# Loading attention's values and later keys, queries and biases from POOL's queue in a one-core hybrid block

## The chip, the core and the metric

The kernel runs on one core of one Trainium2 chip. The metric is the device time of one execution in microseconds (us). A profile of one execution gives the time of every instruction on each engine: TensorE (PE, with its weight loads as PEld), VectorE (DVE), ScalarE (ACT), GpSimd (POOL), and the queue of SyncE (SP), which only starts transfers. Transfers can be started from SP, from ACT and from POOL; they are carried out by the core's 16 DMA engines.

## The reference

One layer of a diffusion backbone over 512 latent tokens (a grid of 8 rows of 64 columns) and 256 context tokens, width 1024. The tokens are normalised and projected; half of the width goes to attention over a neighbourhood and the context (8 heads of 64), the other half to a recurrent scan over time in both directions. Their outputs are joined, projected and added; then a mixture of 32 experts follows. The part at hand, cut:

```
px, pc = hx @ w_in, hc @ w_in
qx, kx, vx = na_heads(px[..., :3 * D_NA], ...)      # latent tokens
qc, kc, vc = na_heads(pc[..., :3 * D_NA], ...)      # context tokens
s_win = (q @ k_band) * scale + bias                 # band of 8 x 32 tokens for 8 x 16 queries
s_ctx = (q @ kc) * scale
p = softmax(concat([s_win, s_ctx]))
o = p[window] @ v_band + p[context] @ vc
```

## The kernel before

The kernel is written in a tile framework: tiles come from pools, the framework places the semaphores, and a planner chooses each queue's order from the program's order and its own estimate of times. Instructions that are pinned (`pin`, or all of TensorE's while `strict` is set) keep the program's order among themselves.

The projections come first. They end with the attention's last values (`nv1`) and queries. Values go to a tensor in memory (NVd, 768 tokens by 512) from ACT's queue; queries (QTd) and keys (KTd) go to memory from SP's, each as a rounded part and a remainder (z = 0, 1).

Then `scan_and_attention` runs two things together on TensorE. The scan has 12 steps (`scan_step(j)`); at the end of step j `scan_load(j + 2)` loads four kinds of tile from SP, into two buffers each, in this order: BKj (pinned, 512 KB), ARz (two halves), UVj (two), TTj. In step j the matmuls `pr`, then `pu`, then `pgr` (which reads BKj and ARz of step j + 1), `pds`, `pgr` again, and the transposes `pkb` (BKj of step j + 1, its last reader). In the gaps of each step the attention is fed in from a generator (`other_work`), in the program's order. The attention has 16 units (`u`): four pairs of heads p, four column blocks cb each. For each unit and head there are the scores `psc` (6 matmuls of k and q), the bias and softmax on VectorE and ScalarE, the transposes `ppt`, and, one unit later, the product with the values `pon` (16 matmuls for both heads).

Its inputs come in two places. `att_values` loads nine V tiles of 128 x 512 (256 KB): seven overlapping bands of the grid, 16 columns of each of the 8 rows, and two of context. Unit 0 uses V0, V2, V7 and V8, the first four issued. `att_load(p)` loads for one pair of heads k, q (rounded), k, q (remainder) and two bias tiles `bt`, 2.0 MB in all; for p = 0 before the scan starts, for p = 1, 2, 3 at the units 2, 6, 10. Even and odd pairs have their own set of buffers. The first two calls also clear the fourth part of `bt` on POOL.

After the attention comes the output projection, with its weights (`wo`, from SP) multiplied by a gate on POOL and split into two parts (`woh`, `wol`), while the scan ends; then the experts, whose weights (384 loads of 512 KB) stream from SP to the end.

Of the kernel before, what the change touches and what calls it, by code (L numbers as in the profile page):

```python
# [226 lines left out]
class K:  # L227
# [1008 lines left out]
    def att_values(s):  # L1236
        nc, PN = s.nc, s.PN
        s.V = {}
        for a in (0, 2, 1, 3, 5, 4, 6):
            s.V[a] = PN.tile([128, 512], F32, name=f"V{a}")  # L1240
            nc.sync.dma_start(s.V[a], s.NV[0:512].rearrange("(r c) f -> r c f", c=64)[:, 8 * a:8 * a + 16])
            if a == 2:
                for b in range(2):
                    s.V[7 + b] = PN.tile([128, 512], F32, name=f"V{7 + b}")
                    nc.sync.dma_start(s.V[7 + b], s.NV[512 + 128 * b:640 + 128 * b])

    def att_load(s, p):

        nc, P = s.nc, s.pns[p % 2]
        t = []  # L1250
        for z in range(2):
            k = P.tile([128, 768], F32, name=f"k{z}")
            s.pin(nc.sync.dma_start(k, s.KTd[p, z]))
            q = P.tile([128, 512], F32, name=f"q{z}")
            nc.sync.dma_start(q, s.QT[p, z])
            t.append((q, k))
        for h in range(2):
            if p < 2:
                s.bt.append(P.tile([128, 4, 256], F32, name=f"bt{h}"))
                nc.gpsimd.memset(s.bt[-1][:, 3], 0.0)  # L1260
            nc.sync.dma_start(s.bt[2 * (p % 2) + h][:, 0:3], s.A['bias'][2 * p + h])
        return t

    def attention(s):
# [730 lines left out]
```

## Time and profile before

| | |
|---|---|
| median of 3 runs | 1205.52 us (1205.4 to 1206.56) |
| the profiled execution's own time | 1203.45 us |
| its span, first to last instruction | 1201.7 us |
| mean granted TensorE clock | 0.956 of full speed |
| TensorE busy | 1105.2 us (92%) |
| VectorE, ScalarE, POOL busy | 658.4, 393.5, 249.6 us |
| DMA moved | 309.98 MB, mean 258 GB/s |

Rows of a timeline give the start, the duration, the engine, the operation with its output and inputs, how many were merged, and in brackets the idle time before and what ended it. The duration of a DMA on a queue is the time to issue it, not to move the data. [...]

### The profile page before, as it was taken

What the parts mean: (1) busy time and instruction counts of PE and PEld (TensorE: products, weight loads), DVE (VectorE), ACT (ScalarE), POOL (GpSimd) and SP (SyncE); (2) the same over time, 40 slices, a digit from 0 to 9 for tenths busy, and PEclk for the clock granted to TensorE, in tenths of its full rate; (3) what the DMA queues carried; (4) which work ended last, traced back from release to release, by engine and by line L of the source; (5) the groups of instructions that cost most, each with busy time, mean ns of one, the idle gap of its engine ahead of it and who ended that gap; (6) DMA issues with size and microseconds to landing.
All of it is one profiled execution on the core that took longest, in us unless ns stands there. A gap on an engine that the chain in (4) does not pass through costs nothing.

```text
span 1201.7 us, 23662 instructions
## 1 busy us (share of the span) xinstructions
PE 1105.2 (92%) x9545; PEld 761.2 (63%) x9546; DVE 658.4 (55%) x1461; ACT 393.5 (33%) x743; POOL 249.6 (21%) x277
## 2 busy tenths in 40 slices
PE   3899988997996798999997979999999999999996
PEld 1677776775764777888775754646464646464644
DVE  5645589659699823554467782333333333333335
ACT  3533551643555344555312252202021111111200
POOL 0654554535244210020135140000000000000000
PEclk9999988997798898999999989999999999999998
DMA  9544634663462488764333939999999999999995
GB/s 366 175 131 128 188 128 137 169 209 98 120 180 102 125 240 220 220 177 107 111 105 101 379 140 352 409 408 409 409 409 409 408 409 408 409 409 409 409 409 187
DMA packets 148764, 309.98 MB, mean 258 GB/s; under 512 B 32291, under 2 KB 71075, under 8 KB 148652
## 3 DMA queue, kind: packets, MB, share of 16 engines
q1 hardware_dynamic: 143868, 306.08, 71.7%
q10 hardware_dynamic: 4752, 2.36, 0.7%
q8 instruction: 76, 1.25, 0.4%
q14 instruction: 36, 0.29, 0.1%
q0 software_dynamic: 32, 0.00, 0.0%
HBM read 283.22 MB, written 25.17 MB: 257 GB/s over the span
## 4 chain that ended last, share of the span: by engine, by line
PE 68%; DVE 21%; DMA 6%; ACT 2%; issue 2%; POOL 1%; SPq 0%; ACTq 0%; DVEq 0%; POOLq 0%
PE ph L242 17%; PE py L242 9%; PE psc L242 7%; PE ipn L242 5%; PE pga L242 5%; PE ip L242 5%; DVE tmp L212 4%; DVE Tc L212 4%; PE pgr L242 2%; DMA wt<-in_w_dram 2%; PE pm L242 2%; PE acc L242 2%; PE pr L242 2%; PE pon L242 1%; PE ppt L246 1%
## 5 line engine op out<-in xcount | busy, mean ns | idle before, releaser
L242 PE MATMUL ph<-wt,HS 128*64 128x512 f32 x1024 | 224.1, 593 | 0.2 <-DMA wt<-in_w_dram 0.2
L242 PEld LDWEIGHTS ph<-wt,HS 128*64 128x64 f32 x1024 | 73.4, 137 | 140.2 <-issue 126.1
L212 DVE TENSOR_TENSOR hid<-hid,ph 128x512 f32<-128x512 f32 x16 | 11.0, 688 | 249.3 <-PE ph L242 249.3
L242 PE MATMUL py<-wt,hid 128*64 128x256 f32 x1024 | 114.5, 381 | 0.0
L242 PEld LDWEIGHTS py<-wt,hid 128*64 128x64 f32 x1024 | 71.9, 137 | 40.3 <-issue 3.9
L212 POOL CAST two<-sel 128x128 fp32r<-128x128 f32 x32 | 8.6, 297 | 425.7 <-PE pbc L242 425.7
L212 POOL TENSOR_TENSOR wlo<-wraw,whi 128x512 fp32r<-128x512 f32 x54 | 74.3, 1378 | 70.2 <-ACT whi L212 67.7
L242 PE MATMUL ipn<-whi,hth 128*128 128x256 f32 x256 | 79.4, 310 | 5.9 <-DVE vs L212 4.8
L212 DVE TENSOR_TENSOR x<-psc,x 128x512 f32<-128x512 f32 (+1 forms) x136 | 78.5, 648 | 0.0
L242 PE MATMUL ip<-hth,whi 128*128 128x512 f32 (+1 forms) x200 | 76.5, 383 | 0.2 <-ACT nr L212 0.2
L242 PE MATMUL ipn<-wlo,hth 128*128 128x256 f32 x256 | 74.7, 292 | 0.0
L242 PE MATMUL ipn<-whi,htl 128*128 128x256 f32 x256 | 74.6, 291 | 0.0
L242 PE MATMUL ip<-htl,whi 128*128 128x512 f32 (+1 forms) x200 | 72.9, 364 | 0.7 <-DVE htl L212 0.7
L242 PE MATMUL ip<-hth,wlo 128*128 128x512 f32 (+1 forms) x200 | 72.5, 363 | 0.0
L242 PEld LDWEIGHTS ipn<-whi,hth 128*128 128x128 f32 x256 | 51.4, 201 | 17.8 <-issue 14.8
L242 PE MATMUL pga<-OH,xh 128*128 128x256 f32 x240 | 60.4, 292 | 0.9 <-DVE OH L212 0.9
L242 PE MATMUL pga<-OH,xl 128*128 128x256 f32 x240 | 59.5, 288 | 0.0
L212 DVE TENSOR_TENSOR tmp<-Mc,Tc 128x30 f32<-128x30 f32 (+14 forms) x120 | 56.8, 473 | 4.8 <-ACT Tc L212 3.2
L242 PE MATMUL psc<-yh,oht 128*128 128x512 f32 (+1 forms) x136 | 54.6, 405 | 1.2 <-DVE x L212 0.8
L212 DVE TENSOR_TENSOR Tc<-Tc,tmp 128x30 f32<-128x30 f32 (+14 forms) x120 | 52.3, 436 | 2.0
L242 PEld LDWEIGHTS ip<-hth,whi 128*128 128x128 f32 x200 | 39.9, 199 | 21.0 <-issue 15.7
L212 ACT ACTIVATE hid<-pth 128x512 f32<-128x512 f32 x16 | 9.6, 599 | 132.7 <-PE pth L246 132.7
(352 smaller groups left out, 2279.6 us busy)
## 6 DMA issues: line engine op xcount, KB each, us to landing
wt<-in_w_dram SPq DMA_DIRECT2D x384, 512.0 KB
wm<-in_wmod_dram SPq DMA_DIRECT2D x48, 512.0 KB
wraw<-in_w_in_dram SPq DMA_DIRECT2D x30, 256.0 KB
wraw<-in_w_na_dram SPq DMA_DIRECT2D x24, 256.0 KB
BKj<-BKd SPq DMA_DIRECT2D x12, 512.0 KB
BKd<-BK SPq DMA_DIRECT2D x12, 384.0 KB
ARz<-ARd SPq DMA_DIRECT2D x16, 256.0 KB
wo<-in_w_out_dram SPq DMA_DIRECT2D x16, 256.0 KB
```

The source lines that it names most:

```text
L212: i = f(*a, **k)
L242: i = s.nc.tensor.matmul(out, l, r, start=start, stop=stop)
L246: i = s.nc.tensor.transpose(out, x, s.ident if ident is None else ident)
```

## The change

Twenty-seven loads name another queue. The nine V loads go from SP to POOL. The six loads of a pair of heads go to POOL for the second, third and fourth pair; the first pair's stay on SP. Sizes, buffers, the order in the program and all other loads are as before.

```
         for a in (0, 2, 1, 3, 5, 4, 6):
             s.V[a] = PN.tile([128, 512], F32, name=f"V{a}")
-            nc.sync.dma_start(s.V[a], s.NV[0:512].rearrange("(r c) f -> r c f", c=64)[:, 8 * a:8 * a + 16])
+            nc.gpsimd.dma_start(s.V[a], s.NV[0:512].rearrange("(r c) f -> r c f", c=64)[:, 8 * a:8 * a + 16])
             if a == 2:
                 for b in range(2):
                     s.V[7 + b] = PN.tile([128, 512], F32, name=f"V{7 + b}")
-                    nc.sync.dma_start(s.V[7 + b], s.NV[512 + 128 * b:640 + 128 * b])
+                    nc.gpsimd.dma_start(s.V[7 + b], s.NV[512 + 128 * b:640 + 128 * b])
...
     def att_load(s, p):
         nc, P = s.nc, s.pns[p % 2]
+        q1 = nc.sync if p == 0 else nc.gpsimd
         t = []
         for z in range(2):
             k = P.tile([128, 768], F32, name=f"k{z}")
-            s.pin(nc.sync.dma_start(k, s.KTd[p, z]))
+            s.pin(q1.dma_start(k, s.KTd[p, z]))
             q = P.tile([128, 512], F32, name=f"q{z}")
-            nc.sync.dma_start(q, s.QT[p, z])
+            q1.dma_start(q, s.QT[p, z])
             t.append((q, k))
         for h in range(2):
...
-            nc.sync.dma_start(s.bt[2 * (p % 2) + h][:, 0:3], s.A['bias'][2 * p + h])
+            q1.dma_start(s.bt[2 * (p % 2) + h][:, 0:3], s.A['bias'][2 * p + h])
         return t
```

## Rows read from the trace of the kernel before

**Rows 1.** The page: busy time (share of span) and instructions; one DMA queue's packets.

```profile
PE 1105.2 (92%) x9545; PEld 761.2 (63%) x9546; DVE 658.4 (55%) x1461; ACT 393.5 (33%) x743; POOL 249.6 (21%) x277
...
q0 software_dynamic: 32, 0.00, 0.0%
```

**Rows 2.** Windows: length, busy time (instructions) per engine, granted clock, DMA share, GB/s.

```profile
440.00:445.00 5.00, 4.44 (x58) 3.59 (x58) 3.15 (x9) 3.72 (x7) 0.00 (x0) 1.00 0.65 159
440.00:458.40 18.40, 14.61 (x202) 11.44 (x201) 9.04 (x26) 10.96 (x22) 0.00 (x0) 0.99 0.83 203
...
449.90:472.20 22.30, 17.10 (x225) 14.79 (x224) 7.86 (x21) 8.61 (x18) 0.00 (x0) 0.85 0.94 233
472.20:487.30 15.10, 15.10 (x225) 13.01 (x224) 8.47 (x23) 10.02 (x21) 0.00 (x0) 1.00 0.55 153
470.00:584.00 114.00, 114.00 (x1695) 96.59 (x1693) 58.23 (x152) 65.45 (x129) 8.15 (x10) 1.00 0.57 156
740.00:760.00 20.00, 20.00 (x122) 8.62 (x119) 4.01 (x7) 1.86 (x3) 0.00 (x0) 1.00 1.03 409
```

**Rows 3.** Timeline of TensorE's matmuls, 432 to 507 us.

```profile
432.23 0.66 PE L246 MATMUL pkb<-cst,BKj 128*128 128x128 f32 x4
...
446.31 1.96 PE L242 MATMUL pon<-PT,V 128*64 128x128 f32 x12
448.54 0.44 PE L242 MATMUL pon<-PT,V 128*64 128x128 f32 x4 [0.27 <-DMA V<-NVd]
...
460.86 1.30 PE L242 MATMUL pgr<-ARz,BKj 128*64 128x128 f32 x5 [5.20 <-DMA BKj<-BKd]
...
462.43 2.07 PE L242 MATMUL pon<-PT,V 128*64 128x128 f32 x13
...
470.18 1.09 PE L242 MATMUL pon<-PT,V 128*64 128x128 f32 x16
...
474.39 0.97 PE L242 MATMUL psc<-k,q 64*128 64x256 f32 x6
...
506.58 0.97 PE L242 MATMUL psc<-k,q 64*128 64x256 f32 x6
```

**Rows 4.** The chain that ended last, in order of time, 440 to 461 us.

```profile
440.85 6.42 DMA V<-NVd
447.29 13.43 DMA BKj<-BKd
```

**Rows 5.** Timeline of SP's queue, 438 to 485 us.

```profile
438.16 1.55 SPq L212 DMA_DIRECT2D ARz<-ARd  x2
440.14 5.65 SPq L212 DMA_DIRECT2D V<-NVd  x9
447.29 0.32 SPq L212 DMA_DIRECT2D BKj<-BKd  x1
...
453.13 0.33 SPq L212 DMA_DIRECT2D k<-KTd  x1
...
460.74 1.30 SPq L212 DMA_DIRECT2D bt<-in_bias_dram  x2
...
484.80 0.43 SPq L212 DMA_DIRECT2D k<-KTd  x1
```

**Rows 6.** Waits of SP's queue, 584 to 665 us: total us, times, longest.

```profile
SPq L212 <- POOL wol L212: 25.4, 5, 6.4
```

**Rows 7.** Timeline of POOL, 437 to 516 us.

```profile
512.60 2.51 POOL L212 TENSOR_TENSOR wo<-wo,g 128x512 f32<-128x512 f32 x2 [75.73 <-DMA wo<-in_w_out_dram]
```

**Rows 8.** Waits of all engines, 395 to 590 us: total us, times, longest.

```profile
PEld pon L242 <- DMA V<-NVd: 1.1, 3, 0.5
```

**Rows 9.** Instructions on tensor cntd, the one transfer issued from POOL.

```profile
L212 POOL DMA_DIRECT2D cntd<-hid x1: 669/669/669, 719.1 to 719.1; - x1
...
DMA to landing us min/median/max: 3.9/3.9/3.9
```

**Rows 10.** Two loads issued from SP: ns of the issue, min/median/max.

```profile
L212 SPq DMA_DIRECT2D brow<-in_bge_dram x1: 283/283/283, 586.6 to 586.6; - x1
...
L212 SPq DMA_DIRECT2D V<-NVd x9: 430/572/669, 440.1 to 445.2; - x9
```

More of the change, by code (lines that the diff above doesn't have):

```diff
@@ L1240, in att_values @@
             s.V[a] = PN.tile([128, 512], F32, name=f"V{a}")
-            nc.sync.dma_start(s.V[a], s.NV[0:512].rearrange("(r c) f -> r c f", c=64)[:, 8 * a:8 * a + 16])
+            nc.gpsimd.dma_start(s.V[a], s.NV[0:512].rearrange("(r c) f -> r c f", c=64)[:, 8 * a:8 * a + 16])
             if a == 2:
@@ L1244, in att_values @@
                     s.V[7 + b] = PN.tile([128, 512], F32, name=f"V{7 + b}")
-                    nc.sync.dma_start(s.V[7 + b], s.NV[512 + 128 * b:640 + 128 * b])
+                    nc.gpsimd.dma_start(s.V[7 + b], s.NV[512 + 128 * b:640 + 128 * b])
     def att_load(s, p):
         nc, P = s.nc, s.pns[p % 2]
+        q1 = nc.sync if p == 0 else nc.gpsimd
         t = []
@@ L1252, in att_load @@
             k = P.tile([128, 768], F32, name=f"k{z}")
-            s.pin(nc.sync.dma_start(k, s.KTd[p, z]))
+            s.pin(q1.dma_start(k, s.KTd[p, z]))
             q = P.tile([128, 512], F32, name=f"q{z}")
-            nc.sync.dma_start(q, s.QT[p, z])
+            q1.dma_start(q, s.QT[p, z])
             t.append((q, k))
@@ L1260, in att_load @@
                 nc.gpsimd.memset(s.bt[-1][:, 3], 0.0)
-            nc.sync.dma_start(s.bt[2 * (p % 2) + h][:, 0:3], s.A['bias'][2 * p + h])
+            q1.dma_start(s.bt[2 * (p % 2) + h][:, 0:3], s.A['bias'][2 * p + h])
         return t
```

## The prediction

> **What bounds the kernel now.** I read the page's engine list first: TensorE is busy for 92% of the span and GpSimd (POOL) for 21% [rows 1]. Averages over stages say nothing about one edit, so next I cut the span into windows [rows 2]. Around the edit the reader is to see two things. From 470 to 584 us TensorE is busy 114.00 of 114 us at full clock: there no load is waited for. Before that, 449.9 to 472.2 and 472.2 to 487.3 hold the same number of matmuls, 225, being two consecutive scan steps with the same attention work between them; the first takes 22.3 us, the second 15.1 us. So about 7.2 us are lost in the first step.
>
> The TensorE timeline says where: 5.20 us of idle time at 455.7, ended by the load of a BKj tile, and slow matmuls behind it (13 matmuls of `pon` take 2.07 us, where 16 of the next group take 1.09) [rows 3]. [...] Hence 7.2 = 5.2 idle + 2.0 at the lower clock.
>
> Why was BKj late? In the chain that ended last, its load takes 13.43 us from 447.29, and before it stands the landing of a V load, 6.42 us from 440.85 [rows 4]. The SP queue's own timeline makes it plain [rows 5]: after the nine V at 440.14 the queue no longer issues freely. BKj goes out when the second V has landed (440.85 + 6.42 = 447.27), eight issues after it. Behind BKj come two UVj, TTj, k, q, k, q and then, eight issues after BKj, `bt` at 460.74, just as BKj lands (447.29 + 13.43 = 460.72). So on SP an issue waits until the load eight places ahead of it has landed.
>
> **The change part by part.**
>
> *V leaves SP.* BKj stands next behind two ARz issues that end at 439.7. The load eight places before it is then one issued before 430, long landed, and the buffer's last reader, the transposes `pkb`, ended at 432.9 [rows 3]. I take the issue at 439.7 instead of 447.3. Even if it again needed 13.4 us it would land at 453.1, before TensorE asks for it at 455.7; it is late again only if it takes longer than the present 13.4 us (rival B). So the wait goes: **-7.2 us**, with the lower clock that followed it. The UVj and TTj behind it go earlier too; TensorE waits for neither today.
>
> *V goes to POOL.* POOL is idle for 75.73 us up to 512.60 [rows 7], so V and the loads behind it delay no arithmetic before the multiplication of `wo`, which serves the output projection after 584. But V itself is on the path: the first `pon` group (16 matmuls from 446.31 to 448.98) takes 2.7 us where a later one takes 1.09, because its weight loads wait for V tiles, three times, 1.1 us in all, the matmuls a little more [rows 3, 8]; the fourth V lands just before the last four matmuls, at about 448.5. Anything that delays the fourth V beyond 448.5 stops TensorE.
>
> What does an issue from POOL cost? The trace has only one, a row of 0.1 KB: 0.67 us, 3.9 us to landing [rows 9]. Lower bound: 0.67 each. Upper: in proportion to packets; that queue moved 32 packets in all [rows 1], a V tile has 128 rows, so 2.7 us. Between them: SP took 0.283 us for a 0.1 KB load and 0.572 for a V [rows 10], a factor of 2.0, which gives 1.35 us on POOL. I take that, since the form differs less from SP's than a plain proportion supposes. Four V are then issued at 440.1 + 5.4 = 445.5, against 442.7 (nine in 5.65 us). If they land as long behind their issue as now (5.9 us for the fourth), the delay is 2.9 us; if only the time behind an issue that the one POOL row shows (3.2 us) and 0.6 us of transfer remain, it is 0.8. BKj is now under way in the same time, 0.5 MB; the DMA share is 0.65 in 440 to 445 [rows 2], so there is room for part of it. I take **+2.0 us**; bounds -1.6 (the present stall gone, since 0.65 leaves room) and, at 2.7 us an issue, 4 x 2.7 - 2.5 = +8.3 (2.5 being what four issues take now).
>
> *k, q and bias of the second pair.* On POOL, behind the nine V. They are first used at 474.4 [rows 3], after the change about 469. Without BKj, UVj and TTj before them they can follow V directly; if POOL too waits eight issues back, k goes when the second V has landed, some 4 us earlier than at present (453.1), and the biases at about 457 instead of 460.7. Some 10 us are left: 0. SP's next BKj no longer stands behind them.
>
> *Third and fourth pair.* The third is issued from 484.80 [rows 5] and first used at 506.58 [rows 3]: 20 us of TensorE's work hide it, and the fourth likewise: 0. SP gets the room, and needs it nowhere, as TensorE does not wait from 470 on.
>
> *Does it last to the end?* From 470 to 584 time is set by TensorE alone, and later the expert weights run at 409 GB/s with all engines busy [rows 2], a stage that begins when TensorE has got there. A shift at 470 should pass to the end undiminished.
>
> Sum: -7.2 + 2.0 = -5.2. The profiled execution took 1203.45 (span 1201.7); it becomes 1198.25. The runs' median is 1205.52, 2.07 above it; so 1205.52 - 5.2 = **1200.3**.
>
> **The rivals.**
>
> *A. V comes sooner, 1196.7.* From 440 to 458.4 the core moved 203 x 18.4 = 3.7 MB [rows 2], while what had landed by then, nine V and two ARz, is 2.6 MB. So 1.1 MB of loads issued later had passed them: V used only part of the engines' width. On another queue that may spread better, and the stall of 1.6 us at 446 goes too: -7.2 - 1.6. [...]
>
> *B. The engines, not the queue, make BKj late: 1205.5.* If V and BKj share so badly that BKj is served last, it lands when all this data has moved, again at about 460.7, and the wait stays. For: the DMA share of 0.94 in that step [rows 2]. Against: 1.1 MB of later loads did pass V, and 0.5 MB at 203 GB/s are 2.6 us. [...]
>
> *C. Slower: POOL writes its loads too slowly.* Place: the first `pon` group. With t us an issue the fourth V is late by 4t - 2.5, and a stall of some us brings the low clock again (2.0). Break-even at t = 1.9; slower by over 2.4 us from t = 2.5. At 2.7: -7.2 + 8.3 + 2.0 = +3.1, 1208.6. [...] Against: the one row of 0.67. [...]
>
> *D. The planner writes another order.* VectorE, ScalarE and SP are ordered by a planner in the output projection; there SP waits 25.4 us for the product `wol`, 6.4 at most once [rows 6]. One more such wait: -5.2 + 6.4 = +1.2, 1206.7.
>
> **How the numbers follow.** What a measurement of this kernel can tell from no change is about 0.2%, 2.4 us. Forecast 0.47, A 0.17, B 0.13, C 0.12, D 0.11 (half of it beyond 2.4 us). Faster: forecast and A, 0.64; same: B and half of D, 0.19; slower: C and half of D, 0.17. The range runs from just under A to just short of C: 1196.5 to 1208. The likeliest case alone: 1198.5 to 1203.
>
> **What would show it.** Right: BKj issued on SP near 440 and no wait of TensorE for it; two steps of nearly equal length; a clock near 1.00 from 450 to 472; V issues on POOL of 1 to 1.5 us; the first `pon` group at 4 to 5 us. Wrong: POOL issues of 2 us or more, with `pon` stopped for longer than 5 us; BKj landing after 455; a wait for `bt` or `k` near 468; or a gain at 470 that is smaller at 660, which would be the planner's.

## The result, and the profile after

The changed kernel takes 1212.95 us (median; 1211.51 to 1213.56) against 1205.46 of the kernel before in the same measurement: ratio 1.0058, 95% interval 1.0036 to 1.008, so 7.5 us slower. The forecast was 1200.3 us and the range ended at 1208.0. The profiled execution took 1211.51 us with a span of 1209.7 us, 8.0 us more than the span before.

What the change was to remove is gone. SP's queue after the change, timeline from 439 to 456 us:

```profile
439.50 0.53 SPq L212 DMA_DIRECT2D BKj<-BKd  x1
440.12 0.38 SPq L212 DMA_DIRECT2D TTj<-TTd  x1
440.74 0.32 SPq L212 DMA_DIRECT2D g<-gated  x1
441.11 1.07 SPq L212 DMA_DIRECT2D wo<-in_w_out_dram  x2
442.29 0.49 SPq L212 DMA_DIRECT2D x<-in_x_dram  x1
443.60 1.39 SPq L212 DMA_DIRECT2D UVj<-VDd  x2
445.03 0.61 SPq L212 DMA_DIRECT2D x<-in_x_dram  x1
455.62 0.33 SPq L212 DMA_DIRECT2D BKj<-BKd  x1
```

BKj goes out at 439.50 and not at 447.29 [rows 5], and TensorE no longer waits for it. But the queue does not stay empty. The gate's vector (`g`, 512 KB), two tiles of output weights (`wo`, 256 KB each) and two of `x` (256 KB each) leave at once, 1.5 MB that serve the output projection, more than 100 us later. In the kernel before, `g` was issued only at 469.75, `wo` at 505.84 and `x` at 511.01.

POOL's queue after the change, timeline from 440 to 470 us:

```profile
440.01 4.98 POOL L212 DMA_DIRECT2D V<-NVd  x8 [14.23 <-DMA QTd<-nx]
447.27 0.59 POOL L212 DMA_DIRECT2D V<-NVd  x1 [2.28 <-DMA V<-NVd]
450.77 0.57 POOL L212 DMA_DIRECT2D k<-KTd  x1 [2.91 <-DMA V<-NVd]
...
465.28 0.54 POOL L212 DMA_DIRECT2D bt<-in_bias_dram  x1 [7.68 <-issue]
...
466.61 2.50 POOL L212 TENSOR_TENSOR wo<-wo,g 128x512 f32<-128x512 f32 x2
```

Eight V take 4.98 us to issue, 0.62 each. Then POOL stands still too: the ninth V, k, k and q each wait for a V to land, and arithmetic queued behind them (the product of `wo` with the gate) comes at 466.61. On the first bias load two views differ: the list of V below puts its 7.7 us on V, the timeline on nothing that it shows (`issue`). Eight places ahead of it stands the sixth V, which by the trace's semaphores had landed at 458.8, 6.5 us before this issue; what held POOL for those 6.5 us stays open. V itself lands late. All instructions on V after the change; first who waited for V (us, times), then issue to landing:

```profile
  POOL bt L212: 7.7, 1
...
  PE pon L242: 5.5, 4
...
DMA to landing us min/median/max: 7.0/13.9/19.7
```

TensorE's matmuls after the change:

```profile
447.03 0.44 PE L242 MATMUL pon<-PT,V 128*64 128x128 f32 x4 [1.16 <-DMA V<-NVd]
450.27 0.44 PE L242 MATMUL pon<-PT,V 128*64 128x128 f32 x4 [2.80 <-DMA V<-NVd]
451.12 0.70 PE L242 MATMUL pon<-PT,V 128*64 128x128 f32 x4 [0.41 <-DMA V<-NVd]
452.99 0.70 PE L242 MATMUL pon<-PT,V 128*64 128x128 f32 x4 [1.18 <-DMA V<-NVd]
```

The first `pon` group stops four times, for 5.5 us, where before it stopped for 0.3 [rows 3]. Windows after the change (columns as in [rows 2]):

```profile
440.00:458.40 18.40, 12.59 (x138) 9.91 (x140) 5.21 (x16) 7.25 (x15) 8.08 (x14) 0.79 1.03 245
...
456.00:458.00 2.00, 2.00 (x38) 1.88 (x38) 0.00 (x0) 0.46 (x1) 0.86 (x2) 0.50 1.15 205
...
464.00:466.00 2.00, 2.00 (x31) 1.88 (x30) 0.33 (x2) 0.00 (x0) 0.72 (x2) 0.50 1.01 387
...
455.50:477.00 21.50, 20.75 (x225) 18.05 (x224) 8.81 (x22) 9.21 (x19) 8.07 (x13) 0.72 1.06 237
477.00:492.20 15.20, 15.20 (x228) 13.07 (x226) 8.54 (x24) 10.13 (x21) 1.03 (x2) 1.00 1.05 255
```

The DMA share in 440 to 458.4 is 1.03 instead of 0.83 [rows 2]. And the step from 455.5, with the same 225 matmuls, is busy for 20.75 of 21.50 us: it waits for almost nothing, yet takes 6.4 us more than the step that needs 15.1 [rows 2]. Its granted clock, a share of full speed, is 0.72: behind the stops for V the clock is 0.50, and stays there while TensorE is busy 2.00 of every 2 us. So 5.65 of the 6.4 us are longer busy time, and 0.75 one wait:

```profile
469.21 0.66 PE L246 MATMUL ppt<-cst,S 128*128 128x128 f32 x4 [0.75 <-ACT S L212]
```

So a pair of losses took the place of the one removed. I count from the start of the `pr` matmuls that read UVj, one group in each step. The table holds every profiled run (first step: the one with the first `pon` group; second: the next; "last V": start of the last four `pon` matmuls of the first group, from the first step's start; empty where they do not stand by themselves).

| kernel | first step | second | third | last V |
|---|---|---|---|---|
| before | 17.11 | 22.30 | 15.10 | 15.72 |
| before, again | 17.30 | 21.88 | 15.11 | 15.90 |
| after | 23.21 | 21.52 | 15.11 | 20.68 |
| after, again | 25.64 | 20.98 | 15.11 | 23.12 |
| values only (e1) | 23.87 | 20.22 | 15.10 | 21.34 |
| keys, queries, biases only (e2) | 24.07 | 20.08 | 15.11 | 21.55 |
| after, other loads held (e3) | 19.49 | 20.82 | 15.11 | 16.97 |
| e3, TensorE kept busy (e5) | 20.53 | 16.37 | 15.10 | 19.13 |
| after, TensorE kept busy (e6) | 24.14 | 29.67 | 15.11 | 22.75 |
| e6, `wo` held (e9) | 24.54 | 15.26 | 26.30 | 23.14 |
| before, BKj ahead of V (e4) | 19.04 | 15.10 | 15.11 | |
| before, BKj fifth (e7) | 16.50 | 15.11 | 18.58 | 15.11 |
| e4, TensorE kept busy (e10) | 17.58 | 15.12 | 16.36 | |

After against before: first step +6.1, second -0.8, together +5.3. In the second pair of profiles it is +8.3 and -0.9, together +7.4.

### The profile page after: what moved, and what is told of

It is laid out like the page before. It is cut to its first block, busy times and chain, and to the rows that moved or that the text cites. A ratio compares the mean times of both kernels' runs of the same rounds, so it can differ in the third digit from the quotient of the medians.

```text
span 1209.7 us, 23692 instructions
## 1 busy us (share of the span) xinstructions
PE 1107.9 (92%) x9545; PEld 763.3 (63%) x9546; DVE 661.2 (55%) x1461; ACT 393.6 (33%) x743; POOL 267.8 (22%) x304
## 4 chain that ended last, share of the span: by engine, by line
PE 66%; DVE 20%; DMA 7%; issue 2%; ACT 2%; POOL 2%; SPq 0%; DVEq 0%; ACTq 0%; POOLq 0%
PE ph L242 17%; PE py L242 8%; PE psc L242 6%; PE ipn L242 6%; PE pga L242 5%; PE ip L242 5%; DVE tmp L212 4%; DVE Tc L212 4%; DMA wt<-in_w_dram 3%; PE pgr L242 2%; PE pm L242 2%; PE acc L242 2%; PE pr L242 1%; PE ppt L246 1%; DMA V<-NVd 1%
## 5 line engine op out<-in xcount | busy, mean ns | idle before, releaser
L242 PEld LDWEIGHTS ipn<-whi,hth 128*128 128x128 f32 x256 | 51.3, 200 | 18.1 <-issue 15.1
```

The costliest lines, as they stand in the source:

```text
L242: i = s.nc.tensor.matmul(out, l, r, start=start, stop=stop)
```

## The experiments

The first four runs had three theories: T1, the freed SP queue sends other loads early, and these crowd V out of the DMA engines; T2, a load issued from POOL is itself slow to land; T3, another order of the planner costs time later, in the output projection.

**Values only (e1), and the rest only (e2).** Against the changed kernel: e1 keeps k, q and biases on SP (the first edit below); e2 keeps V on SP (the second, and the same for the two V of context).

```diff
-        q1 = nc.sync if p == 0 else nc.gpsimd
+        q1 = nc.sync
```
```diff
-            nc.gpsimd.dma_start(s.V[a], s.NV[0:512].rearrange("(r c) f -> r c f", c=64)[:, 8 * a:8 * a + 16])
+            nc.sync.dma_start(s.V[a], s.NV[0:512].rearrange("(r c) f -> r c f", c=64)[:, 8 * a:8 * a + 16])
```

> Only the nine V loads move to POOL; keys, queries and biases of all pairs stay on SP. Theory T1 (the freed SP queue starts other loads early and these crowd V out of the DMA engines): SP now starts k, q, k, q of the second pair at about 441, 1.3 MB beside V instead of the gate, wo and x, so the first pon group still takes 5 us or more and the clock falls; 1207 to 1212 us. Theory T2 (a load from POOL is itself slow to land): the same group takes 6 us or more whatever SP does; 1210 to 1213. Both expect no wait for BKj.

> Only keys, queries and biases of the second to fourth pair move to POOL; V stays on SP, so BKj still goes out behind V. T1: the wait of 5.2 us for BKj stays and the first pon group keeps its 2.7 us, unless POOL's loads, early, crowd V: 1205 to 1209, the clock loss after 456 as in the kernel before. T2: the V loads are on SP, so nothing is lost: 1205. A third theory, T3 (the planner's other order of wo and x costs 3 us of its own between 606 and 630): 1208.

Measured: e1 1211.41 us against 1204.43, ratio 1.0052 (1.0034 to 1.007); e2 1210.9, ratio 1.0052 (1.0031 to 1.0073). Either half alone costs as much as both. In e1, SP sent the second pair's k, q, k, q from 441.42, and TensorE waited 5.7 us for V. e2 is the sharper one, since V is issued from SP there as before. POOL's timeline in e2:

```profile
435.49 0.73 POOL L212 DMA_DIRECT2D k<-KTd  x1 [10.63 <-PE ipn L242]
...
438.83 0.54 POOL L212 DMA_DIRECT2D bt<-in_bias_dram  x1
```

SP's queue in e2:

```profile
440.19 10.29 SPq L212 DMA_DIRECT2D V<-NVd  x9
```

and TensorE's waits in e2, 440 to 480 us (total us, times, longest):

```profile
PE pon L242 <- DMA V<-NVd: 6.0, 3, 5.0
```

Two MB for the second pair were under way before the first V, and V was late from SP's own queue. Part of that lies in the issues themselves, 10.29 us for nine V against 5.65 before [rows 5]. V's lateness therefore does not need POOL: whichever queue has nothing in front of it starts loads that nobody needs yet (2.0 MB from POOL here, 1.5 MB from SP in the changed kernel). That speaks for T1 and against T2 as the main cause. The wait for BKj, which the expectation had stay, is gone although BKj went out only at 451.39: TensorE came to it later.

**The freed queue held back (e3).** The change, with `g`, the first two `wo` and `x` pinned to a late place on SP (the last argument of `wout` pins its load; the loads of `x` are moved here from the output projection's setup).

```diff
             if u == 5:
-                s.nc.sync.dma_start(s.g1, s.gate[0:1].to_broadcast([128, 1024]))
+                s.pin(s.nc.sync.dma_start(s.g1, s.gate[0:1].to_broadcast([128, 1024])))
+            if u == 9:
+                for i in (3, 2, 1, 0):
+                    for h, c in enumerate((i, 7 - i)):
+                        s.pin(s.nc.sync.dma_start(s.x1[64 * h:64 * h + 64, i], s.A['x'][64 * c:64 * c + 64]))
             if u == 14:
-                s.wpre = [s.wout(k, 0, s.POW, 2) for k in range(2)]
+                s.wpre = [s.wout(k, 0, s.POW, 2, True) for k in range(2)]
```

> The changed kernel, but the loads of the gate, of the first two wo tiles and of x are pinned on SP behind the scan's loads (x at unit 9), so that SP starts only BKj, TTj and UVj (1.0 MB) beside V. T1: V lands in time, the first pon group takes 2.5 to 4.5 us, no low clock, the second scan step takes 15 to 16 us; 1198 to 1203 us. T2: the pon group still takes 6 us or more, with the low clock behind it; 1208 to 1213. T3 is untouched by the first stretch: 3 us between 606 and 630 go or stay with the order of wo.

Measured: 1207.2 us against 1204.43 (runs from 1195.55 to 1211.07), ratio 1.0011 (0.9983 to 1.0038), so the slowdown is mostly gone. All instructions on V in e3, issue to landing:

```profile
DMA to landing us min/median/max: 6.1/9.9/11.6
```

TensorE's timeline in e3:

```profile
448.70 1.37 PE L242 MATMUL pon<-PT,V 128*64 128x128 f32 x12 [1.39 <-DMA V<-NVd]
450.72 0.70 PE L242 MATMUL pon<-PT,V 128*64 128x128 f32 x4 [0.64 <-DMA V<-NVd]
```

V lands in 9.9 us instead of 13.9, and the last `pon` matmuls begin 1.3 us later than before, not 5.0 (table). So T1 holds for V. In e5 below, which holds the same loads, the last `pon` matmuls begin 3.4 us later than before; its V, issue to landing:

```profile
DMA to landing us min/median/max: 7.4/11.4/13.3
```

The 1.3 to 3.4 us that are left can be T2 or the sharing with BKj, TTj and UVj; no run separates them. T1's forecast failed beyond V: the second step stayed at 20.82 us, at a low clock, and the time missed 1198 to 1203. Windows of e3:

```profile
452.00:454.00 2.00, 2.00 (x21) 1.67 (x21) 0.00 (x0) 1.50 (x3) 0.00 (x0) 0.50 1.13 184
...
464.00:466.00 2.00, 2.00 (x20) 2.00 (x19) 1.35 (x3) 0.56 (x2) 0.00 (x0) 0.50 1.09 246
```

Two waits of 2.0 us in all were followed by a clock of 0.50 from 450 to 466 us.

**BKj first, all on SP (e4).** The kernel before with the third step's BKj and ARz issued, pinned, ahead of V and no longer at the end of the first step.

```diff
+        if j == 0:
+            f = lambda t: t.rearrange("p d a b -> p (d a) b")
+            s.pin(nc.sync.dma_start(f(s.BK2[0]), f(s.BK[2])))
+            for h in range(2):
+                r = slice(64 * h, 64 * h + 64)
+                s.pin(nc.sync.dma_start(s.ARz[0][r, :, :, h, 0:64].rearrange("p d a b -> p (d a) b"), f(s.AR[2])[r, :, 0:64]))
```

> The kernel before, all on SP, with one thing moved: BKj and ARz of the third step are issued before V instead of behind it. This measures the term of -7.2 us by itself. If it holds, no wait for BKj, the second step takes 15.1 us, V lands up to 2.5 us later because 0.5 MB now goes ahead of it, 1198 to 1202 us. If the engines' load and not the queue's order sets these waits, V's delay eats it: 1204 to 1207.

Measured: 1199.06 us, ratio 0.9945 (0.9926 to 0.9964): 0.55% faster than the kernel before. Window of e4's second step:

```profile
452.00:467.10 15.10, 15.10 (x225) 13.01 (x224) 7.85 (x21) 8.39 (x18) 0.00 (x0) 1.00 0.92 248
```

The step lost its 7.2 us. V came later, behind BKj's and ARz's transfers, which cost the first step 1.9 us (a wait of 1.1 and the low clock behind it, 0.59 and 0.56 from 448 to 452 us). That this is nearly the +2.0 that the prediction had for V is chance. 7.2 - 1.9 = 5.3, and the third step begins 5.1 us earlier.

For the next runs the question was the clock. In their expectations "theory C" is: what is lost behind a late V is the low clock; D: late operands; E: the clock falls whatever TensorE does; F: POOL's queue itself holds up the second step. (They are not the prediction's rivals of the same letters.)

**e3 with TensorE kept busy (e5), the change with TensorE kept busy (e6).** Extra matmuls, overwritten by the real ones, ahead of the first `pon` group: 12 in e5, 26 in e6.

```diff
             po[p] = s.ps(tag='rm', name="pon")
+            if p == 0:
+                w = s.kp[0][0][0].bitcast(F32R)
+                for _ in range(12):
+                    s.mm(po[p], w[:, 0:128], w)
```

> e3_hold with 12 more matmuls (a query tile with itself, 128 x 512 each) into the values' product of the first pair just ahead of the real ones; what they write is overwritten, so the output is as before and 2.9 us or so of TensorE work is added. It keeps TensorE busy while V is awaited. Theory C (what e3_hold still pays, although its values' products end only 0.6 us later than before's, is the stretch of granted clock 0.50 that follows): the clock stays at 1.00 after the first values' products, the second step takes about 15.1 us instead of e3's 20.8, and the time is 1200 to 1202. Rival D (the step is long because its own operands come late, from POOL's queue): the step stays near 20 us with waits on loads in it, and the time stays at 1207 or above. Rival E (the clock falls anyway): granted clock 0.50 for some 15 us all the same, 1207.

> The changed kernel with 26 such extra matmuls (about 6.2 us of TensorE work, overwritten) ahead of the first pair's values' products, and nothing else moved. V comes as late as in the changed kernel. Theory C: the values' products still end some 5 us later than in the kernel before, but the clock stays at 1.00 behind them, and the second step is about 15 us instead of 21.5: some 6 us less than the changed kernel, 1206 to 1207. Theory E (the clock falls anyway) or D (late operands): 1213, as the changed kernel.

e5 took 1200.32 us against 1205.33, ratio 0.9952 (0.9936 to 0.9969). (The 0.6 us in its expectation is 1.3 counted from the step's own start.) Window of e5's second step:

```profile
451.90:468.20 16.30, 15.27 (x225) 12.95 (x224) 7.85 (x21) 7.95 (x17) 4.47 (x10) 1.00 1.06 270
```

With 2.9 us of useless work added, the kernel became 6.9 us faster than e3 (medians; each against its own runs of before: 1.0011 to 0.9952), as the clock stayed at 1.00. That is theory C. One caution: its runs spread from 1196.31 to 1204.21 us and overlap e3's, the profiled execution took 1203.19, and the two steps of the profile show 3.4 us less than e3's, not 6.9.

e6 took 1219.05 us, ratio 1.0107 (1.0087 to 1.0126): worse than the change. The clock did stay at 1.00 behind the `pon` group, but a new wait came. TensorE in e6:

```profile
473.13 1.12 PE L246 MATMUL ppt<-cst,S 128*128 128x128 f32 x4 [11.42 <-ACT PT L212]
```

ACT in e6:

```profile
470.74 0.63 ACT L212 ACTIVATE woh<-wo 128x512 fp32r<-128x512 f32 x1 [19.34 <-POOL wo L212]
```

POOL in e6:

```profile
468.11 0.54 POOL L212 DMA_DIRECT2D bt<-in_bias_dram  x1 [7.86 <-issue]
...
469.44 2.49 POOL L212 TENSOR_TENSOR wo<-wo,g 128x512 f32<-128x512 f32 x2
```

Read from the bottom: the bias load stands on POOL for 7.86 us, for which the timeline names nothing (`issue`), as in the changed kernel; the product of `wo`, arithmetic, is queued behind it; ACT's `woh`, which the planner had put ahead of the softmax's PT, `wo` coming early, waits for it; TensorE waits for PT. The same chain is in the changed kernel, at a lower price: ACT waits 4.57 us for `wo` at 467.92, and TensorE 0.75 for the S that ACT makes next.

**e6 with `wo` held (e9).** As e6, with the two `wo` pinned as in e3; `g` and `x` still come early.

> e6_after_warm (the changed kernel with 26 extra matmuls, overwritten, ahead of the first pair's values' products) with one thing more: the first two loads of the output weights (wo) keep their written place, so that ACT has no rounding of them (woh) among the softmax's work; the gate's vector and x still come early. In e6_after_warm the clock stayed at 1.00, as theory C said, but ACT stood 19 us before woh, behind POOL, which stood behind its own loads, and TensorE waited 11.4 us for ACT. Theory C (of the changed kernel's second step, 6.4 us are low clock): no such wait here, the second step takes 15 to 16.5 us at 1.00, and with V still some 4 to 5 us late the time is 1204 to 1207. Rival F (POOL's queue itself holds up the second step: the loads of pair two are late, or another operation takes woh's place): the second step stays above 19 us at clock 1.00, 1210 or more.

Measured: 1212.09 us against 1205.09, ratio 1.0064 (1.004 to 1.0088). Windows of e9's second and third step:

```profile
457.90:473.10 15.20, 15.20 (x225) 12.96 (x224) 7.85 (x21) 7.94 (x17) 3.23 (x7) 1.00 1.05 228
473.10:499.40 26.30, 18.28 (x226) 15.39 (x224) 8.40 (x23) 10.37 (x21) 2.16 (x5) 0.81 0.97 223
```

TensorE's waits in e9, 455 to 500 us:

```profile
PE pgr L242 <- DMA ARz<-ARd: 7.6, 1, 7.6
```

The second step takes 15.3 us at clock 1.00, as theory C said, against 21.5: 6.2 us less, of which 0.75 at most are the wait behind `woh`, gone as well, and the rest the low clock. The time is not as low as theory C said, and rival F, which had 1210 or more, had it for another reason. The next step waits 7.6 us for ARz and then runs at the low clock itself, 0.50 from 484 to 492 us. By the program's order this is the ARz issued from 460.13 on, 27 us before it was there. With DMA shares of 1.05 and 0.97 I read it so: the early loads had only pushed the lateness on, and when TensorE is faster it meets the next load sooner. e5, which holds `g`, `wo` and `x` all, has no such wait and a third step of 15.10 us.

**BKj fifth (e7).** The kernel before, all on SP; only the third step's BKj moves, behind the four V that unit 0 needs (the V are pinned for that).

```diff
                 for b in range(2):
                     s.V[7 + b] = PN.tile([128, 512], F32, name=f"V{7 + b}")
-                    nc.sync.dma_start(s.V[7 + b], s.NV[512 + 128 * b:640 + 128 * b])
+                    s.pin(nc.sync.dma_start(s.V[7 + b], s.NV[512 + 128 * b:640 + 128 * b]))
+                f = lambda t: t.rearrange("p d a b -> p (d a) b")
+                s.pin(nc.sync.dma_start(f(s.BK2[0]), f(s.BK[2])))
```

> The kernel before with every load on SP's queue; only the load of the third step's coefficients (BKj) is moved, from behind the nine loads of V to the fifth place, behind V0, V2, V7 and V8 and ahead of the other five. If the price of e4_bk_first was V's delay (1.4 to 2 us), the values' products here end as in the kernel before, the 5.2 us wait on BKj is gone, the second step is 15 us, and the time is 7 us below the kernel before, 1198. If the five later V are needed as early as the first four, it is 1199 to 1200, as e4_bk_first. If eight loads in flight on one queue are what delays BKj wherever it stands, BKj is still awaited and the time stays at 1205.

Measured: 1200.45 us, ratio 0.9957 (0.9941 to 0.9972). TensorE in e7:

```profile
446.82 0.44 PE L242 MATMUL pon<-PT,V 128*64 128x128 f32 x4 [0.24 <-DMA V<-NVd]
...
471.14 1.30 PE L242 MATMUL pgr<-ARz,BKj 128*64 128x128 f32 x5 [2.12 <-DMA ARz<-ARd]
```

The first step is not longer than before and the second takes 15.11 us, the whole 7.2 us; 3.5 of it go in the third step, to a wait for ARz and the clock behind it (0.61 and 0.54 from 470 to 474 us). As I read it, this is e9 again: this load stream is nearly full (DMA share 1.09 to 1.17 from 464 to 470 us) and gives part of the gain back at its next item.

**e4 with TensorE kept busy (e10).** Eight extra matmuls, as in e5.

> e4_bk_first (all loads on SP's queue, the third step's coefficients ahead of V) with 8 of the extra matmuls (1.9 us of TensorE work, overwritten) ahead of the values' products. There V was 1.1 us late and some 2.5 us ran at granted clock 0.50 behind it. Theory C: the clock stays at 1.00, the first step is about 1 us shorter, and the time is 1198, 1 us below e4_bk_first. If low clock costs nothing there, the extra matmuls cost what V's lateness does not cover, and it is 1199 to 1200.

Measured: 1205.22 us (1198.81 to 1213.71), ratio 1.0 (0.9977 to 1.0022), 6 us worse than e4. The first step did become shorter (17.58 against 19.04), but the planner, with other times to plan by, moved `wo` forward on SP (487.76) and `woh` on ACT, and the step from 481.62 took 23.49 us (17.09 in e4). TensorE in e10:

```profile
501.31 1.97 PE L242 MATMUL pon<-PT,V 128*64 128x128 f32 x14 [4.22 <-ACT PT L212]
```

ACT in e10:

```profile
500.14 0.63 ACT L212 ACTIVATE woh<-wo 128x512 fp32r<-128x512 f32 x1 [5.12 <-POOL wo L212]
```

So the expectation's arithmetic held in the place it spoke of and failed 40 us later. e6 and e10 share the pattern: `woh` ahead of PT.

**Both kernels again (e8, e11).**

> The kernel before, unchanged, for a second profile. The stretch of the output projection that takes 23.3 us in the profiled run of the kernel before and 26 to 28 us in those of the changed kernel and three of the four experiments: if that stretch varies from run to run by itself, it is 26 us or more here in the same kernel; if it is a cost of the change, it is 23.3 again.

> The changed kernel again, for a second profile. If the late V and the low clock behind it belong to the change, both are here: TensorE waits for V 4 to 6 us in the first step, the second step takes 20 us or more with most of it at granted clock 0.50, and the third begins 4 us or more after that of the kernel before. The stretch of the output projection (27.8 us in the first profile, 23.3 and 26.4 us in two profiles of the kernel before) may come out anywhere from 23 to 28.

e8 took 1203.41 us, e11 1212.63. In e11 TensorE waits 7.5 us for V, the second step takes 20.98 us and the third begins at 478.28: the losses belong to the change. In the kernel before, the stretch of the output projection took 23.3 us in the first profile; in e8 its first and last `pr` are

```profile
605.25 1.15 PE L242 MATMUL pr<-UVj,Gj 64*64 64x64 f32 x32
631.66 1.15 PE L242 MATMUL pr<-UVj,Gj 64*64 64x64 f32 x32
```

26.4 us apart, and e8's span is again 1201.7 us. T3 falls: that stretch differs by 3 us between two executions of one unchanged kernel, with the same span.

## Why the prediction was wrong

**The 7.2 us were right.** BKj was issued at 439.50, as predicted, nothing waits for it, and where V is not late (e7) the second step takes 15.11 us. Rival B falls.

**The +2.0 us for V had the wrong cause and the wrong size.** The prediction put it down to the price of an issue on POOL, 1.35 us. Eight in a row took 0.62 each, below even the lower bound of 0.67, and by the prediction's own formula V would not have been later at all. It was 5.0 us later (7.4 in e11). The step that failed is the one left out: what SP sends in the room that it gets. "SP gets the room, and needs it nowhere" was said of TensorE's needs; the planner fills the room all the same. 1.5 MB (1.57 million bytes) at the 245 GB/s of that window are 6.4 us of the engines' time (an estimate), and holding the loads back took 3.7 of the 5.0 us away (e3), and 3.6 of 7.0 between e6 and e5. The share of 0.65 "leaves room" only while nobody else takes it: in the same 5 us it was 0.97 after the change. Rival D had the planner, but looked for it in the output projection. Nor did a second queue keep loads out of each other's way: in e2 TensorE waited 6.0 us for V, issued just after POOL's 2.0 MB, though V never left SP.

**The low clock behind a stop was sized at 2.0 us, and in the forecast not at all.** Of the 6.4 us that the second step was too long (21.5 against 15.1), 5.65 are the low clock and 0.75 the wait behind `woh`; e9 without either takes 6.2 less. The 2.0 (17.10 us busy against 15.10 [rows 2]; in the kernel before the clock was 0.53, 0.50, 0.50 and 0.77 in the windows of 2 us from 458 to 466 us) came from the one stop in the trace, and there was no reason that the next would cost the same: behind 5.2 us of idle time before the clock was back within the step, behind 2.0 us in e3 it stayed low for 16 us.

So the forecast's -7.2 + 2.0 reads, as measured in the first two steps: -7.2 for BKj, +6.1 in the first step (V, and the clock's beginning), +6.4 in the second (5.65 for the clock): +5.3. Rival C came nearest, 1208.6, with the right place (the first `pon` group) and its two terms, a late V and a low clock, but its condition, issues of 2.7 us on POOL, is refuted at 0.62, so that its number is luck. Rival A falls: on POOL's queue V never came sooner than in the kernel before (last V at 16.97 us or later, against 15.72 and 15.90), and no run shows a better spread there.

**"V and the loads behind it delay no arithmetic" failed too.** It rested on POOL's 75.73 us of idle time [rows 7], a row of an order that the change rewrites: with `wo` early, its product stands on POOL at 466.61 behind the biases. In the change that goes with a wait of 0.75 us on TensorE, in e6 with 11.4. The biases themselves, forecast at about 457, began at 465.28; TensorE did not wait for them.

**"Undiminished to the end"** can't be confirmed. The medians differ by 7.5 us, the steps by 5.3 in one pair of profiles and 7.4 in the other. From the `pr` near 606 us to the end the profiles of before took 595.65 and 596.45 us, those of after 598.90 and 598.57, and those of the experiments between 593.2 and 599.3 with no tie to V or the clock. So 3.3 of the 8.0 us between the first two spans lie in the last half, and 2.1 of the 9.2 between the second two; their cause stays open.

The change's idea has a value once its side effects are held: e5, with every load on the queue the change gave it, the other loads held and extra matmuls, takes 1200.32 us. But e4 reaches 1199.06 us on SP alone by moving one load ahead, without extra work.

## What to carry to other kernels

Moving loads to another queue frees the old one, and a planner fills it, here with 1.5 MB: before counting the gain, ask which loads come next there, how many bytes they are and whose transfers they join. If one load stands behind others in a queue, reorder the queue first; a second queue removes the order that protected the urgent loads (here the last V came 5.0 us later). Price a stop of TensorE with the clock behind it (here 5.65 us in the step behind 5.5 us of stops), from several stops and not from one, and look for the next load that a faster engine will meet.

## What the runs showed of the hardware

- A load of 128 rows from POOL's queue takes 0.54 to 0.80 us to issue (V after the change: median 0.66, eight in a row 4.98), with VectorE busy for 2.80 of those 5 us. The one row of before took as long (0.67 us for 0.1 KB [rows 9]): the price did not grow with the rows.
- POOL, like SP (BKj at 447.29, the second V landed at 447.27 [rows 4, 5]), stood when a load eight places back had not landed (2.28 us before the ninth V), and arithmetic queued behind it stood with it (the product of `wo` at 466.61, behind a bias load at 465.28). It also stood 6.3 to 7.9 us before the first bias load in five runs that issue it behind V from POOL (after, e3, e5, e6, e9); after the change the sixth V had landed 6.5 us before that load went out. The cause is open.
- The time at the low clock did not follow the length of the stop. Clock 0.50 lasted some 17 us with 5.5 us of stops (after) and with 2.0 us (e3), 3.4 us with a stop of 1.1 us (e4), and 6.8 us with one of 5.2 (before), added up from windows of 2 us. In the first two TensorE was busy 2.00 of 2 us through most of it. With 12 or 26 extra matmuls ahead of the `pon` group the clock stayed at 1.00 through stops of 1.6 to 2.4 us for V (e5, e6, e9).
- The nine V from POOL landed in 13.9 and 14.3 us (median; after, e6) with `g`, `wo` and `x` beside them, and in 9.9 and 11.4 us (e3, e5) without.
